# Merging the transfers of a transfer-bound LoRA projection, and sending three small stores from GpSimd earlier

## Chip, cores, metric

One core of a Trainium2 chip. The metric is the device time of one execution in microseconds, of the slowest core (here the only one). Lower is better. The profile's span, from the first to the last instruction, is about 1.3 us shorter than this time.

## The reference

```python
# x: 16 x 2048 x 256, W: 256 x 256, lora_A: 256 x 16, lora_B: 16 x 256, lora_E: 16, scale = 1
x_flat = x.reshape(-1, in_dim)              # 32768 rows of 256 floats
y = x_flat @ W
lora_out = ((x_flat @ lora_A) * lora_E) @ lora_B
return (y + scale * lora_out).reshape(batch, seq_len, out_dim)
```

The kernel folds the low-rank part into one matrix, W + A diag(E) B, and then does one multiplication per row. It must read 33.55 MB of x and write 33.55 MB of y.

## The kernel before

The rows are cut into four chunks of 64 rows on each of 128 partitions, and each chunk into 16 groups of 4 rows. There are three homes in SBUF (chunk 3 goes into the home of chunk 0). For each group GpSimd casts four rows to bf16 (`stage`), TensorE transposes them, VectorE copies the transposed words out, TensorE multiplies, and ScalarE writes the result over the input in the home. The sync engine sends loads and large stores in the order of one list:

```python
ORDER = [
    ("A",),
    ("L", 0, 0, 8), ("L", 0, 8, 24), ("L", 0, 24, 40), ("L", 0, 40, 64),
    ("L", 1, 0, 32), ("L", 1, 32, 64),
    ("L", 2, 0, 16), ("L", 2, 16, 64),
    ("S", 0, 0, 40), ("S", 0, 40, 64),
    ("L", 3, 0, 32), ("L", 3, 32, 64),
    ("S", 1, 0, 64), ("S", 2, 2, 62), ("S", 3, 0, 64),
]
SHARED = 2                       # of chunk 2, the first and last 2 rows ...
SHARES = (slice(108, 113), slice(0, 108), slice(113, P))   # ... go out from GpSimd's queue
HELD = (2, 16)                   # GpSimd holds this group until ...
HOLDERS = (("S", 0, 0, 40),)     # ... this store has landed
```

A store's semaphore makes the load that overwrites its home wait. The end of GpSimd's program and TensorE's loop:

```python
def gpsimd_program():
    # ... identity, then for g in range(N_GROUPS): waits, the hold, and
        gpsimd.tensor_copy(out=stage[g % NS][:], in_=home(c)[:, b:b + CG, :]).then_inc(s_stage[g % UNROLL], 1)

    gpsimd.wait_ge(s_turned, N_GROUPS - NS + 1)
    gpsimd.drain().then_inc(s_stage[N_GROUPS % UNROLL], 1)   # the last release
    gpsimd.wait_ge(s_shared, 1)
    for p in SHARES:
        share(gpsimd, p, shared_stored)                      # a DMA start each

def tensor_program():
    # ...
    with tensor.Fori(0, N_GROUPS // UNROLL):
        for i in range(UNROLL):
            turn(i + 1, i)      # waits for s_stage of group i + 1
            multiply(i)
```

In the loop TensorE transposes group i + 1 before it multiplies group i. After group 63 there is no group 64, yet the loop still does `turn(64)` on old data and throws the result away. The drain, an instruction without data that serves here only to raise a semaphore, is the last release. So **group 63 is multiplied only after the drain has ended**.

Of the kernel before, what the change touches and what calls it, by code (L numbers as in the profile page):

```python
# [16 lines left out]

ORDER = [
    ("A",),
    ("L", 0, 0, 8),  # L20
    ("L", 0, 8, 24),
    ("L", 0, 24, 40),
    ("L", 0, 40, 64),
    ("L", 1, 0, 32),
    ("L", 1, 32, 64),
    ("L", 2, 0, 16),
    ("L", 2, 16, 64),
    ("S", 0, 0, 40),
    ("S", 0, 40, 64),
    ("L", 3, 0, 32),  # L30
    ("L", 3, 32, 64),
    ("S", 1, 0, 64),
    ("S", 2, 2, 62),
    ("S", 3, 0, 64),
]

SHARED = 2
END_ROWS = 2
SHARES = (slice(108, 113), slice(0, 108), slice(113, P))

HELD = (2, 16)
HOLDERS = (("S", 0, 0, 40),)

WARM_UP = 2

EARLIER = 5

CG = 4
GPC = ROWS // CG
# [8 lines left out]
def kernel(  # L58
# [41 lines left out]
        for op in ORDER  # L100
        if op[0] == "S" and (op in HOLDERS or op[1] < N_CHUNKS - N_HOMES)
    }
    stored = {op: sem(f"stored_{op[1]}_{op[2]}") for op in ORDER if op in waited}
    s_shared = sem("shared_done")
    shared_stored = sem("shared_stored")
# [13 lines left out]
    def home(c):  # L119
        return homes[c % N_HOMES]  # L120

    sync, gpsimd, scalar, vector, tensor = nc.sync, nc.gpsimd, nc.scalar, nc.vector, nc.tensor
# [41 lines left out]
    def share(engine, p, landed):  # L164
        def ends_of(rows):
            return rows[p].rearrange("p (q b) k -> p q b k", b=END_ROWS)[:, :: ROWS // END_ROWS - 1, :, :]

        engine.dma_start(out=ends_of(y_chunks[SHARED]), in_=ends_of(home(SHARED))).then_inc(landed, 16)  # L168

    def gpsimd_program():  # L170
        gpsimd.memset(ident[:], 0.0).then_inc(s_ident, 1)  # L171
        gpsimd.wait_ge(s_ident, 1)
        gpsimd.affine_select(  # L173
            out=ident[:],
            in_=ident[:],
            compare_op=ALU.not_equal,
            fill=1.0,
            base=0,
            pattern=[[-1, P]],
            channel_multiplier=1,  # L180
        ).then_inc(s_ident, 1)
        for g in range(N_GROUPS):
            c, b = g // GPC, g % GPC * CG
            for op, landed in loaded.items():
                if op[1:3] == (c, b):
                    gpsimd.wait_ge(landed, 16)
            if (c, b) == HELD:
                for op in HOLDERS:
                    gpsimd.wait_ge(stored[op], 16)
            if g >= NS:  # L190
                gpsimd.wait_ge(s_turned, g - NS + 1)  # L191
            gpsimd.tensor_copy(out=stage[g % NS][:], in_=home(c)[:, b:b + CG, :]).then_inc(s_stage[g % UNROLL], 1)  # L192

        gpsimd.wait_ge(s_turned, N_GROUPS - NS + 1)
        gpsimd.drain().then_inc(s_stage[N_GROUPS % UNROLL], 1)
        gpsimd.wait_ge(s_shared, 1)
        for p in SHARES:
            share(gpsimd, p, shared_stored)

    def scalar_program():  # L200
        for name, to, of in (
            ("w", w_sb, W.rearrange("(q t) m -> q t m", t=KT)),
            ("b", b_sb, lora_B),
            ("e", e_sb, lora_E[:, None]),
        ):
            ins = scalar.dma_start(out=to[:], in_=of).then_inc(set_up_loaded[name], 16)
            opening.append(ins.ins.name)
        for g in range(N_GROUPS):
            c, b = g // GPC, g % GPC * CG
            scalar.wait_ge(s_y, g + 1)  # L210
            scalar.copy(out=home(c)[:, b:b + CG, :], in_=psum_y[g % NY][:]).then_inc(s_free[(g + NY) % UNROLL], 1)  # L211
            if (c, b + CG) == (SHARED, ROWS):
                scalar.drain().then_inc(s_shared, 1)
            if g in ends:
                scalar.drain().then_inc(s_done, 1)  # L215

    def vector_program():
        vector.wait_ge(set_up_loaded["e"], 16)
        vector.wait_ge(s_pe_set_up, 1)
        vector.tensor_scalar(  # L220
            out=ate[:],
            in0=psum_y[0][:R, :KT, :P],
            scalar1=e_sb[:],
            scalar2=float(scale),
            op0=ALU.mult,
            op1=ALU.mult,
        ).then_inc(s_ate, 1)
        for g in range(N_GROUPS):
            vector.wait_ge(s_turned, g + 1)
            vector.tensor_copy(out=xt[g % NX][:], in_=psum_xt[g % NT][:].bitcast(BF16)).then_inc(s_xt[g % UNROLL], 1)  # L230
            if g == 0:
                vector.wait_ge(set_up_loaded["w"], 16)
                vector.wait_ge(s_pe_set_up, 2)
                vector.tensor_add(out=weff[:], in0=w_sb[:], in1=psum_y[1][:, :KT, :]).then_inc(s_free[0], 1)  # L234
                vector.drain().then_inc(s_free[1], 1)
                for _ in range(EARLIER):
                    vector.drain()

    def tensor_program():
# [54 lines left out]
    with tc.tile_critical(no_gpsimd_drain=True):  # L294
        sync_program()
        gpsimd_program()
        scalar_program()
        vector_program()
        tensor_program()
# [35 lines left out]
```

## Time and profile before

| | before |
|---|---|
| time, median of 6 runs | 161.64 us (161.13 to 163.21) |
| profiled execution | 160.84 us, span 159.5 us |
| bytes over HBM | 67.4 MB, mean 423 GB/s |
| last cast on GpSimd, last copy on ScalarE | 112.6 us, done at 118.4 us |
| drain on GpSimd | at 113.9 us, 46 ns |
| the three shares: first issue, landing of the last | 114.7 us, 147.4 us |
| first packet of store 3 | 138.5 us |

The page's line for the main queue (q1) and the strip of 40 slices are read in the prediction. The point to keep in mind is that the first packet of store 3 (138.5 us) comes 20 us after the last copy (118.4 us): that is slack in which something may grow unseen.

### The profile page before, as it was taken

Reading aid. Unit: us, or ns where it says so; the run is one execution under the profiler, and the core shown is the slowest. Engines: PE = TensorE matmul, PEld = TensorE weight load, DVE = VectorE, ACT = ScalarE, POOL = GpSimd, SP = SyncE. Lnnn points to the kernel's source line nnn. Section 1 sums busy time; section 2 is a strip of 40 time slices with the busy share of each in tenths; the row PEclk is TensorE's granted clock in tenths of the full one; section 3 lists DMA queues with packets and bytes.
Section 4 is the critical chain, followed back from the end, with each engine's and each line's share of the span. In section 5 each row is a group of like instructions: output and inputs, shape, how many; then the busy total and the mean of one; then the engine's idle time right before and its main releaser. Section 6 shows DMA issues by size and latency. Waiting matters only on the chain.

```text
span 159.5 us, 2034 instructions
## 1 busy us (share of the span) xinstructions
PE 93.8 (59%) x782; PEld 82.4 (52%) x782; DVE 45.4 (28%) x66; ACT 66.1 (41%) x65; POOL 68.8 (43%) x73
## 2 busy tenths in 40 slices
PE   2969969959999990000899999999940000000000
PEld 1349959959999990000789999999930000000000
DVE  0145534525555550000135555555500000000000
ACT  3025775747777772000147777777750000000000
POOL 1537838377777740001557777787620000000000
PEclk9999999999999999655569999999995555555555
DMA  7999999999999997999999999989979979969896
GB/s 257 417 440 466 401 460 394 501 419 394 431 423 542 444 394 320 431 401 436 413 477 411 411 468 435 536 362 427 493 327 480 502 308 484 514 297 540 378 411 263
DMA packets 2739, 67.43 MB, mean 423 GB/s; under 512 B 544, under 2 KB 560, under 8 KB 816
## 3 DMA queue, kind: packets, MB, share of 16 engines
q1 hardware_dynamic: 2304, 66.60, 97.5%
q0 software_dynamic: 224, 0.52, 0.9%
q10 hardware_dynamic: 208, 0.28, 0.5%
q14 instruction: 3, 0.02, 0.0%
HBM read 33.85 MB, written 33.55 MB: 423 GB/s over the span
## 4 chain that ended last, share of the span: by engine, by line
DMA 43%; PE 27%; POOL 1%; ACT 1%; SPq 1%; issue 0%; ACTq 0%; POOLq 0%
DMA out_dram<-home 30%; PE psum_y L259 17%; DMA home<-in_x_dram 12%; PE psum_xt L248 9%; POOL stage L192 1%; ACT home L211 1%; SPq L156 0%; ACTq L215 0%; SPq L330 0%; POOLq L191 0%; SPq L294 0%
## 5 line engine op out<-in xcount | busy, mean ns | idle before, releaser
L211 ACT COPY home<-psum_y 128x1024 f32<-128x1024 f32 x64 | 64.8, 1012 | 50.3 <-PE psum_y L259 50.3
L192 POOL CAST stage<-home 128x1024 bf16<-128x1024 f32 x64 | 66.1, 1040 | 44.8 <-DMA out_dram<-home 17.3
L259 PE MATMUL psum_y<-weff,xt 128*128 128x256 bf16 x512 | 68.1, 277 | 0.0
L230 DVE COPY xt<-psum_xt 128x1024 bf16<-128x1024 bf16 x64 | 44.3, 692 | 62.7 <-PE psum_xt L248 62.6
L259 PEld LDWEIGHTS psum_y<-weff,xt 128*128 128x128 bf16 x512 | 51.0, 100 | 5.8
L248 PE MATMUL psum_xt<-ident,stage 128*128 128x128 f32 x260 | 40.7, 280 | 20.6 <-POOL stage L192 20.2
L248 PEld LDWEIGHTS psum_xt<-ident,stage 128*128 128x128 f32 x260 | 31.3, 145 | 23.4 <-issue 22.0
L272 PE MATMUL psum_y<-ident 128*128 128x512 f32 x4 | 3.8, 1101 | 2.9 <-POOL ident L173 2.9
L272 PEld LDWEIGHTS psum_y<-ident 128*128 128x128 f32 x4 | 1.2, 325 | 3.9 <-POOL ident L173 2.9
L220 DVE TENSOR_SCALAR ate<-psum_y,e_sb 16x256 f32<-16x256 f32 x1 | 0.5, 472 | 7.2 <-PE psum_y L275 7.2
L168 POOL DMA_DIRECT2D out_dram<-home x3 | 2.0, 675 | 1.0 <-PE psum_xt L248 1.0
L211 ACT ACT_TABLE_LOAD x1 | 1.3, 1283 | 2.0 <-SPq L294 2.0
L281 PE MATMUL psum_y<-b_sb,ate 16*128 16x256 f32 x4 | 1.1, 393 | 0.1
L171 POOL MEMSET ident<- 128x128 f32 x1 | 0.2, 204 | 1.7 <-SPq L294 1.7
L275 PEld LDWEIGHTS psum_y<-ident,a_sb 128*16 128x16 f32 x2 | 0.3, 138 | 1.2 <-issue 1.2
L281 PEld LDWEIGHTS psum_y<-b_sb,ate 16*128 16x128 f32 x4 | 0.7, 184 | 0.4 <-issue 0.3
L234 DVE TENSOR_TENSOR weff<-w_sb,psum_y 128x512 bf16<-128x512 f32 x1 | 0.7, 686 | 0.6 <-PE psum_y L281 0.6
L275 PE MATMUL psum_y<-ident,a_sb 128*16 128x128 f32 x2 | 0.6, 421 | 0.0
L173 POOL TENSOR_SCALAR_AFFINE_SELECT ident<-ident 128x128 f32<-128x128 f32 x1 | 0.3, 283 | 0.2 <-POOL ident L171 0.2
L316 POOL MEMSET const-float32-0.0<- 128x1 f32 x1 | 0.1, 93 | 0.2 <-issue 0.2
L316 POOL MEMSET const-bfloat16-1.0<- 128x1 bf16 x1 | 0.1, 95 | 0.0
L316 POOL MEMSET const-uint8-127<- 128x1 uint8 x1 | 0.1, 95 | 0.0
(1 smaller groups left out, 0.1 us busy)
## 6 DMA issues: line engine op xcount, KB each, us to landing
home<-in_x_dram SPq DMA_DIRECT2D x4, 4096.0 KB, 24.2
out_dram<-home SPq DMA_DIRECT2D x1, 7680.0 KB, 42.3
home<-in_x_dram SPq DMA_DIRECT2D x3, 2048.0 KB, 13.0
home<-in_x_dram SPq DMA_DIRECT2D x1, 6144.0 KB, 58.2
out_dram<-home SPq DMA_DIRECT2D x1, 5120.0 KB, 48.3
home<-in_x_dram SPq DMA_DIRECT2D x1, 3072.0 KB, 19.9
out_dram<-home SPq DMA_DIRECT2D x1, 3072.0 KB, 45.9
home<-in_x_dram SPq DMA_DIRECT2D x1, 1024.0 KB, 5.4
```

The source lines that it names most:

```text
L168: engine.dma_start(out=ends_of(y_chunks[SHARED]), in_=ends_of(home(SHARED))).then_inc(landed, 16)
L192: gpsimd.tensor_copy(out=stage[g % NS][:], in_=home(c)[:, b:b + CG, :]).then_inc(s_stage[g % UNROLL], 1)
L211: scalar.copy(out=home(c)[:, b:b + CG, :], in_=psum_y[g % NY][:]).then_inc(s_free[(g + NY) % UNROLL], 1)
L220: vector.tensor_scalar(out=ate[:], in0=psum_y[0][:R, :KT, :P], scalar1=e_sb[:], scalar2=float(scale), op0=ALU.mult, op1=ALU.mult,).then_in ...
L230: vector.tensor_copy(out=xt[g % NX][:], in_=psum_xt[g % NT][:].bitcast(BF16)).then_inc(s_xt[g % UNROLL], 1)
L234: vector.tensor_add(out=weff[:], in0=w_sb[:], in1=psum_y[1][:, :KT, :]).then_inc(s_free[0], 1)
L248: ins = tensor.transpose(psum_xt[i % NT][:, b, :], words[:, b, :], ident[:])
L259: ins = tensor.matmul(psum_y[i % NY][:, b, :], xt[i % NX][:, b, t::KT], weff[:, t, :], start=(t == 0), stop=(t == KT - 1),)
L272: tensor.matmul(psum_y[1][:, :2, :], ident[:], ident[:, None, :].to_broadcast([P, 4, P]), start=True, stop=True)
L275: ins = tensor.transpose(psum_y[0][:R, t, :P], a_sb[:, t, :], ident[:])
L281: ins = tensor.matmul(psum_y[1][:, t, :], ate[:, t, :], b_sb[:], start=True, stop=True)
L316: nc = _bacc.Bacc("TRN2", target_bir_lowering=False, num_devices=1)
```

## The change

The intent, as far as the change shows it, is to send as few transfers as fit: fewer and larger loads, store 0 whole, 24 rows of store 1 ahead of load 3 to keep the queue fed while load 3 waits for store 0. The three shares go out in the middle of chunk 3, not at the end. Some drains shift the places of the instruction fetches.

```diff
 ORDER = [
     ("A",),
-    ("L", 0, 0, 8),
-    ("L", 0, 8, 24),
-    ("L", 0, 24, 40),
+    ("L", 0, 0, 16),
+    ("L", 0, 16, 40),
     ("L", 0, 40, 64),
     ("L", 1, 0, 32),
     ("L", 1, 32, 64),
-    ("L", 2, 0, 16),
-    ("L", 2, 16, 64),
-    ("S", 0, 0, 40),
-    ("S", 0, 40, 64),
-    ("L", 3, 0, 32),
-    ("L", 3, 32, 64),
-    ("S", 1, 0, 64),
+    ("L", 2, 0, 64),
+    ("S", 0, 0, 64),
+    ("S", 1, 0, 24),
+    ("L", 3, 0, 64),
+    ("S", 1, 24, 64),
     ("S", 2, 2, 62),
     ("S", 3, 0, 64),
 ]
+SHARED_AT = (3, 16)
-HELD = (2, 16)
-HOLDERS = (("S", 0, 0, 40),)
+HELD = (2, 0)
+HOLDERS = (("S", 0, 0, 64),)
-EARLIER = 5
+VECTOR_DRAINS = 9
+GPSIMD_DRAINS = 7
+SCALAR_DRAINS = 15
# (cut: one loop of drains each at the start of GpSimd and ScalarE; VectorE's loop had 5)
@@ gpsimd_program
+            if (c, b) == SHARED_AT:
+                gpsimd.wait_ge(s_shared, 1)
+                for p in SHARES:
+                    share(gpsimd, p, shared_stored)
             if g >= NS:
                 gpsimd.wait_ge(s_turned, g - NS + 1)
             gpsimd.tensor_copy(...)

         gpsimd.wait_ge(s_turned, N_GROUPS - NS + 1)
         gpsimd.drain().then_inc(s_stage[N_GROUPS % UNROLL], 1)
-        gpsimd.wait_ge(s_shared, 1)
-        for p in SHARES:
-            share(gpsimd, p, shared_stored)
```

The order on GpSimd: before, drain and then shares; after, shares and then drain.

More of the change, by code (lines that the diff above doesn't have):

```diff
@@ L181, in gpsimd_program @@
         ).then_inc(s_ident, 1)
+        for _ in range(GPSIMD_DRAINS):
+            gpsimd.drain()
         for g in range(N_GROUPS):
@@ L207, in scalar_program @@
             opening.append(ins.ins.name)
+        for _ in range(SCALAR_DRAINS):
+            scalar.drain()
         for g in range(N_GROUPS):
@@ L235, in vector_program @@
                 vector.drain().then_inc(s_free[1], 1)
-                for _ in range(EARLIER):
+                for _ in range(VECTOR_DRAINS):
                     vector.drain()
```

## The prediction

> **What bounds the kernel now.** I read the page's queue table first, then the strip of 40 slices, then the chain of waits, then the table by stage, then the sync engine's own waits and GpSimd's timeline.
>
> ```profile
> DMA packets 2739, 67.43 MB, mean 423 GB/s; under 512 B 544, under 2 KB 560, under 8 KB 816
> q1 hardware_dynamic: 2304, 66.60, 97.5%
> HBM read 33.85 MB, written 33.55 MB: 423 GB/s over the span
> ...
> DMA  7999999999999997999999999989979979969896
> ```
>
> 33.55 MB of x must come in and 33.55 MB of y go out. The main queue alone fills 97.5% of the time of 16 DMA engines. The digits below 9 in the strip are mostly an artefact, since a long packet is counted in the slice where it starts. Laying the packet records of the trace on one clock, I find 15 to 16 or more packets in flight at every instant from 2.0 us to 158.4 us of a 159.5 us span. No engine of DMA is idle between those two times. So the kernel is bound by transfer time and nothing else; compute matters only if it makes a transfer start late.
>
> ```profile
> core 0: us, PE busy (x) PEld busy (x) DVE busy (x) ACT busy (x) POOL busy (x), PEclk, DMA share, GB/s
> ...
> 2.00:20.00 18.00, 15.78 (x101) 11.34 (x102) 6.69 (x10) 7.43 (x8) 10.53 (x12) 1.00 1.02 428
> 20.00:58.00 38.00, 34.82 (x318) 31.96 (x316) 17.99 (x27) 26.69 (x27) 26.95 (x27) 1.00 1.02 442
> 58.00:62.00 4.00, 2.14 (x20) 1.71 (x18) 1.38 (x2) 2.59 (x3) 0.00 (x0) 1.00 1.00 342
> 62.00:80.00 18.00, 3.74 (x18) 3.15 (x19) 0.74 (x2) 0.91 (x1) 3.09 (x4) 0.59 0.97 417
> 80.00:99.00 19.00, 19.00 (x166) 17.42 (x165) 9.63 (x14) 13.26 (x14) 14.30 (x14) 0.94 1.00 432
> ```
>
> The DMA share (last but one column) stays near 1 in every stage, whether TensorE is busy or idle. One stage is poor in bytes: 342 GB/s at 58 to 62 us, where the first store follows the last load of chunk 2. There the trace shows some 17 packets of 49152 B taking 2.4 to 2.9 us instead of 1.82; the excess of that size group, divided by 16, is 0.86 us. The later changes between loads and stores (at 81 and 100 us) show next to none.
>
> ```profile
> SPq L156 <- DMA out_dram<-home: 38.3, 1, 38.3
> POOL stage L192 <- DMA out_dram<-home: 17.3, 1, 17.3
> ...
> 75.08 2.02 POOL L192 CAST stage<-home 128x1024 bf16<-128x1024 f32 x2 [17.32 <-DMA out_dram<-home]
> 112.61 1.04 POOL L192 CAST stage<-home 128x1024 bf16<-128x1024 f32 x1 [0.27 <-PE psum_xt L248]
> 114.69 2.02 POOL L168 DMA_DIRECT2D out_dram<-home  x3 [1.04 <-PE psum_xt L248]
> ```
>
> The long waits are deliberate or harmless. GpSimd holds chunk 2 for 17.3 us until the first store has landed (74.97 us), and the sync engine waits for the same store before it sends the first load of chunk 3 into that home. Meanwhile the second store of chunk 0 (24 rows) keeps the queue fed. The chain of waits runs through these holds and through TensorE (27%), but TensorE finishes at 117.4 us, and the last store's first packets start at 138.5 us: some 20 us of slack that the share in the chain hides.
>
> **What the Trainium skill says.** "DMA: Bandwidth & Descriptors", section "Where 436 GB/s comes from", puts the ceiling of the SBUF ports at 435 GB/s. The trace agrees: a 65536 B packet takes 2418 ns, 27.1 B/ns, or 434 GB/s for 16 engines; the 358 GB/s that the page gives as the HBM limit does not bind here (mean 423). The same page, section "Anatomy of one DMA", gives a fixed cost of about 2 us per DMA, mostly the wait for the completion receipt. That is no queue time here: packets of consecutive transfers follow each other without a hole, so merging transfers saves descriptor overhead, not 2 us each. Section "Queues, rings and completion order" says each engine takes its queues in turn, packet by packet; the trace agrees, the GpSimd queue's 4096 B packets start 2.42 us apart on each engine, one after each 61440 B packet (2267 + 159 ns). "TensorE: Matmul & The Clock Gate", section "What's actually happening", has the clock halve after an idle window and recover after some 3.4 us of work; the trace shows half clock from 65.2 to 82.2 us, with work resumed at 76.3, so about 6 us to recover here.
>
> **The change, part by part.**
>
> Removed: three transfers of the main queue. Before has four loads of chunk 0, two each of chunks 1, 2 and 3, and five stores, 15; after has 3 + 2 + 1 + 1 loads and 5 stores, 12. Each transfer gives every engine 8 packets, one per partition, and one semaphore write. Durations in the trace: 309 ns for 8192 B, 611 for 16384, 1213 for 32768, 2418 for 65536. The slope is (2418 - 309) / 57344 = 0.0368 ns per byte, so 8192 B are 301 ns and the fixed part of a packet is 8 ns. Per transfer and engine: 8 x 8 ns + 9 ns (the 4 B write) = 0.07 us. Three fewer: 0.21 us, all of it on the bound.
>
> Start: the first load doubles from 8 to 16 rows. Its first packet still starts at about 2.0 us. The first 8-row load loses 0.22 us per engine to company (packets of up to 662 ns instead of 309), mostly the weights' packets; some of that company's cost may go, I take 0.05 us. Compute begins later by 8 rows x 0.30 us = 2.4 us; nothing waits for it, since the first store is due only when the loads end at about 61 us.
>
> Moved: store 0 whole, then 24 rows of store 1 ahead of load 3. I lay the queue out with 0.3015 us a row (64 rows: 8 x 2.418 = 19.3 us). Loads 0 to 2 end at about 61.1 us (if the 0.86 us stays). Store 0 ends at 80.5 and lands at about 80.9. The 24 rows last 24 x 0.3015 = 7.2 us, to 87.8. Load 3 waits for store 0's landing, so it is sent at about 81 with nearly 7 us to spare, the same margin as now. Its end is 107.1; the 40 rows of store 1 end at 119.2, store 2's 60 rows at about 137.5, and store 3 follows.
>
> Compute has to fit into this. Chunk 2 is released at 80.9 instead of having four groups done early. The four first casts at half clock cost 82.48 - 75.08 = 7.4 us, the rest 1.31 us each: the 16th cast starts at 80.9 + 7.4 + 11 x 1.31 = 102.7, and its result is in SBUF 5.8 us later (as 112.61 to 118.4 now), at 108.5. Store 2 is due at 119.2: 10 us to spare. Chunk 3 lands at about 107.5. Sixteen groups: three casts in 3.1, twelve steps of 1.31 (15.7), plus the three shares now sent by GpSimd in the middle (2.0 us, and 0.8 before it as now between the drain at 113.9 and the first at 114.7), plus 5.8: 107.5 + 3.1 + 15.7 + 2.8 + 5.8 = 134.9. Store 3 is due when the first engine gets there, about 137.5 to 138.5. So the slack shrinks from 20 us to about 3, yet stays above zero.
>
> The shares' packets now start at about 114 instead of 119.6; they are the same 128 packets (1.4 us per engine in the mean) and still end well before the end.
>
> Drains: 15 on ScalarE, 7 on GpSimd, 4 more on VectorE (10 ns each there, issued 40 ns apart). All stand in stretches where these engines wait for loads; cost zero. They move the instruction stream, and so the three 8192 B instruction fetches at 61.7, 80.0 and 102.7 us. Each costs one engine 309 ns; at most the engine that ends last gains that.
>
> Sum: -0.21 - 0.05 - about 0.1 for fetches and the end's unevenness (the engines' last packets end between 158.4 and 159.15 us) = about -0.35 us of 159.5. I set it against 161.66, whose three runs lie at 161.13, 161.66 and 163.21, so its middle may be high by 0.1: 161.2 us.
>
> **The rivals.** First, a hole before store 3, because slack falls to 3 us: if the clock stays halved through chunk 3 (2.5 us a group instead of 1.31), its results come about 19 us late and the time grows by some 15 us, to 177. Against it: TensorE pauses only about 1 to 3 us between chunks 2 and 3, and the trace keeps full clock through a 2.9 us wait for a load at 32.6 us. A milder form, 1 to 2 us late, makes 162 to 163. Second, the slow changeover at 58 to 62 us vanishes or grows with 65536 B packets and a whole store: without it, the time is 160.3. For this: the later changeovers cost nothing. Against it: it belongs to the first store, which comes in the same place after the same loads. Third, a different spread over the engines: in before, one engine's eight packets of store 1 take 2564 ns each, 146 more than the rest, 1.2 us in all, which the uneven shares seem to make good. If after has the slowness on another engine, the end moves by up to 1.2 us, to 162.4.
>
> **Range and chances.** The bound is 67.1 MB at 434 GB/s, 154.6 us, and the fixed start (2.0), end and launch (1.3 us between time and span) leave no road to 158.4, which 2% faster would need: 0.01. Slower by over 2% needs a hole of 3.2 us: 0.03. The range is the run-to-run spread plus rivals two and three: 160.1 to 162.5.
>
> **What would show it.** The main queue should have 2304 - 3 x 144 = 1872 packets (128 data and 16 semaphore writes each). DMA packets should stay in flight without a hole from 2 to 158 us; TensorE's last matmul should fall at about 134 and the last store's issue before 137; the hold on GpSimd should run to about 81 us. A pause of the queue around 87 us (load 3 late) or 138 us (store 3 late) would prove me wrong on the slack; a DMA rate near 430 GB/s around 60 us would show that the changeover went.

## The result, and the profile after

The changed kernel takes 167.47 us (median of 6, 167.21 to 168.01) against 161.64 us: **ratio 1.0354**, 95% interval 1.0309 to 1.0399, slower. A ratio here is the mean time of one kernel's fast runs over that of the other's fast runs of the same rounds, so it is not quite the ratio of the medians quoted. The prediction was 161.2 us with a range to 162.5.

First the page's queue lines and the strip, after:

```profile
DMA packets 2307, 67.43 MB, mean 406 GB/s; under 512 B 496, under 2 KB 512, under 8 KB 768
q1 hardware_dynamic: 1872, 66.60, 93.8%
...
DMA  7999998989799796999799799889998992099595
GB/s 276 436 432 432 420 474 387 489 387 568 316 505 505 286 458 300 474 489 442 322 414 592 302 474 489 367 385 454 508 414 352 497 483 92 0 505 505 253 505 253
```

The packets are exactly the 1872 predicted, and the bytes are the same. But the main queue's share falls from 97.5% to 93.8%, and slices 34 and 35 of the strip (a slice is 4.15 us) show 92 and 0 GB/s. The transfers stop when store 2 has ended. The table by stage gives the place; first before, then after (the last two columns are the DMA share and GB/s):

```profile
138.00:140.00 2.00, 0.00 (x0) 0.00 (x0) 0.00 (x0) 0.00 (x0) 0.00 (x0) 0.50 1.35 574
140.00:146.00 6.00, 0.00 (x0) 0.00 (x0) 0.00 (x0) 0.00 (x0) 0.00 (x0) 0.50 0.85 360
```

```profile
138.00:140.00 2.00, 0.00 (x0) 0.00 (x0) 0.00 (x0) 0.00 (x0) 0.00 (x0) 0.75 0.40 158
140.00:146.00 6.00, 2.79 (x12) 1.92 (x12) 0.00 (x0) 1.01 (x1) 0.00 (x0) 0.50 0.00 1
146.00:164.00 18.00, 0.00 (x0) 0.00 (x0) 0.00 (x0) 0.00 (x0) 0.00 (x0) 0.50 1.08 466
```

From 140 to 146 us next to nothing is moved (1 GB/s), and TensorE does 12 matmuls: the 4 transposes of the pass that is thrown away and the 8 products of group 63. Nearly everywhere else the packet records again show 16 or more in flight. Summed over the time from 138 to 148 us, the 16 DMA engines stand idle 6.5 us each in the mean, which is the whole difference of the spans (166.0 - 159.5). So the question is what holds the last group back. The chain of waits of the changed kernel, in that window (start, duration, what):

```profile
132.87 0.87 PE psum_y L264 x8
133.74 0.45 PE psum_xt L253 x4
134.19 7.03 POOLq L201
141.22 0.14 issue
141.36 1.09 PE psum_xt L253 x4
142.45 1.72 PE psum_y L264 x8
144.17 0.02 issue
144.19 1.01 ACT home L216
```

L201 is the drain on GpSimd. The chain puts 7.03 us on it. By the timeline TensorE's last other product, of group 62, ended at 135.06 us, and TensorE then sat idle for 6.31 us. Then come the pass that is thrown away, the product of group 63 (both at half clock by now: 1.72 us against 0.87 for the product), ScalarE's copy, and store 3, sent at 145.26 us into an empty queue. The same line looked at by itself, after and then before:

```profile
L201 POOLq DRAIN  x1: 8308/8308/8308, 132.9 to 132.9; - x1
...
  PE psum_xt L253: 6.3, 1
```

```profile
L195 POOLq DRAIN  x1: 46/46/46, 113.9 to 113.9; - x1
```

The drain grew from 46 ns to 8308 ns. By the Trainium skill, "Perfetto Trace Analysis", section "Per-engine timelines", the profiled time of a drain starts only when its semaphores are satisfied. The trace agrees: it starts at 132.91 us, when TensorE has done the transposes that it was told to wait for. So the 8.3 us are not the wait written in the program. What ends them is next to them in the trace: the last of the 48 increments of the shares' semaphore comes at 141.04 us, and the drain ends at 141.22.

### The profile page after: what moved, and what is told of

Its sections match the earlier page's. It is cut to its first block, busy times and chain, and to the rows that moved or that the text cites. A ratio compares the mean times of both kernels' runs of the same rounds, so it can differ in the third digit from the quotient of the medians.

```text
span 166.0 us, 2053 instructions
## 1 busy us (share of the span) xinstructions
PE 98.2 (59%) x782; PEld 85.2 (51%) x782; DVE 45.4 (27%) x66; ACT 66.1 (40%) x65; POOL 69.0 (42%) x73
## 3 DMA queue, kind: packets, MB, share of 16 engines
q1 hardware_dynamic: 1872, 66.60, 93.8%
## 4 chain that ended last, share of the span: by engine, by line
DMA 49%; PE 29%; POOLq 4%; POOL 4%; ACT 1%; issue 1%; SPq 0%; ACTq 0%
DMA out_dram<-home 28%; DMA home<-in_x_dram 21%; PE psum_y L264 17%; PE psum_xt L253 11%; POOLq L201 4%; POOL stage L198 3%; ACT home L216 1%; PE psum_y L286 1%; POOL out_dram L168 1%; SPq L147 0%; ACTq L220 0%
## 5 line engine op out<-in xcount | busy, mean ns | idle before, releaser
L264 PE MATMUL psum_y<-weff,xt 128*128 128x256 bf16 x512 | 70.2, 283 | 0.0
L253 PE MATMUL psum_xt<-ident,stage 128*128 128x128 f32 x260 | 42.9, 291 | 43.1 <-POOL stage L198 36.8
L253 PEld LDWEIGHTS psum_xt<-ident,stage 128*128 128x128 f32 x260 | 32.6, 150 | 46.3 <-issue 45.0
L264 PEld LDWEIGHTS psum_y<-weff,xt 128*128 128x128 bf16 x512 | 52.1, 102 | 6.8
L286 PE MATMUL psum_y<-b_sb,ate 16*128 16x256 f32 x4 | 2.1, 670 | 0.0
L286 PEld LDWEIGHTS psum_y<-b_sb,ate 16*128 16x128 f32 x4 | 1.2, 320 | 0.5 <-issue 0.3
```

The lines of the kernel that those rows point to most:

```text
L253: ins = tensor.transpose(psum_xt[i % NT][:, b, :], words[:, b, :], ident[:])
L264: ins = tensor.matmul(psum_y[i % NY][:, b, :], xt[i % NX][:, b, t::KT], weff[:, t, :], start=(t == 0), stop=(t == KT - 1),)
L286: ins = tensor.matmul(psum_y[1][:, t, :], ate[:, t, :], b_sb[:], start=True, stop=True)
```

## The experiments

Theory A: GpSimd's drain waits until the transfers that GpSimd itself has started have landed. Theory B: whatever GpSimd runs after starting transfers is held. Theory C: the drain is a symptom, and holding chunk 2 until the whole of store 0 has landed leaves too little slack. All kernels gave correct results. "Before" had medians of 161.46 us (e1 to e4) and 161.48 (e5 to e8).

**e1: the release by a memset.**

```diff
# changed kernel
+    scratch = sbuf("scratch", [P, 1], FP32)
-        gpsimd.drain().then_inc(s_stage[N_GROUPS % UNROLL], 1)
+        gpsimd.memset(scratch[:], 0.0).then_inc(s_stage[N_GROUPS % UNROLL], 1)
```

> The changed kernel with one instruction replaced: GpSimd's last release (the one that lets TensorE run its last pass) is a memset of 128x1 in place of the drain. Theory A, the drain waits until GpSimd's own share transfers have landed (141.04 us in the trace, the drain ends at 141.22): the release falls at about 133 us, the last copy ends at about 136.6, store 3 is in the queue before store 2 ends (about 139), the hole is gone, time 160.8 to 161.4. Theory B, anything that GpSimd runs after its transfers is held by them: memset held too, 167.4. Theory C, the slack was simply too small because chunk 2 is held longer: a hole stays, 163 or more.

162.12 us (161.20 to 162.37), ratio to before 1.0024 (0.9987 to 1.0061): the loss is gone. The memset's line, then the stages at the place of the hole:

```profile
L202 POOL MEMSET scratch<- x1: 98/98/98, 132.8 to 132.8; 128x1 f32 x1
```

```profile
138.00:140.00 2.00, 0.00 (x0) 0.00 (x0) 0.00 (x0) 0.00 (x0) 0.00 (x0) 1.00 0.97 408
140.00:146.00 6.00, 0.00 (x0) 0.00 (x0) 0.00 (x0) 0.00 (x0) 0.00 (x0) 0.55 0.98 420
```

The memset runs at 132.84 us, while the shares land at 141.81. B falls, and C falls as an explanation of this loss: with all of the new order kept, the queue has no hole (15 or more packets in flight from 2 to 157 us). The time is 0.7 us above the expected upper bound; see the last part of this section.

**e2: the shares after the drain again.** All else as changed.

```diff
# changed kernel
-            if (c, b) == SHARED_AT:
-                gpsimd.wait_ge(s_shared, 1)
-                for p in SHARES:
-                    share(gpsimd, p, shared_stored)
 ...
         gpsimd.drain().then_inc(s_stage[N_GROUPS % UNROLL], 1)
+        gpsimd.wait_ge(s_shared, 1)
+        for p in SHARES:
+            share(gpsimd, p, shared_stored)
```

> The changed kernel with the three share transfers sent after the drain again, as before the change; all else (order of transfers, drain counts, hold) as changed. Theory A: drain of 0.05 us, hole gone, about 161.0; the shares land near 150 to 155 us, ahead of the end. Theory C: GpSimd saves only the 2 to 3 us that the shares took in the middle, so time stays above 164.

162.04 us, ratio 1.0026 (0.9992 to 1.0061). The drain takes 39 ns at 131.2 us; the last share lands at 159.45, close to the end of store 3 and not at 150 to 155 us as I had expected, and the time is 1.0 us above the expected one. The new order of loads and stores, the longer hold and the added drains together are thus within noise of before.

**e3: the kernel before, with the shares early and nothing else.**

```diff
# kernel before
+SHARED_AT = (3, 16)
+            if (c, b) == SHARED_AT:            # in the loop over groups, as in the change
+                gpsimd.wait_ge(s_shared, 1)
+                for p in SHARES:
+                    share(gpsimd, p, shared_stored)
 ...
         gpsimd.drain().then_inc(s_stage[N_GROUPS % UNROLL], 1)
-        gpsimd.wait_ge(s_shared, 1)
-        for p in SHARES:
-            share(gpsimd, p, shared_stored)
```

> The kernel before with the shares sent after four groups of chunk 3 and the drain after them, nothing else. Theory A: the drain, now at about 116 us, is as long as the shares are still under way (until about 122 to 128 us), yet store 3 is due only at 138.5, so the time stays within 0.5 of 161.6. Theory B or C: drain of 0.05 us, or no drain effect; same time. The length of the drain, not the time, tells them apart.

161.91 us, ratio 1.0012 (0.9961 to 1.0063). Its drain:

```profile
L200 POOLq DRAIN  x1: 20593/20593/20593, 115.2 to 115.2; - x1
...
  PE psum_xt L250: 18.6, 1
```

The drain takes **20.6 us**, more than twice that of the changed kernel, and the time does not move clear of noise: the last copy ends at 139.80 us, just about when store 3 falls due. The 20 us of slack are used up and a little more: by the packet records of this trace the first packet of store 3 starts at 140.69 us, and the 16 DMA engines stand idle for 1.0 us each in the mean before it. The shares were under way until 135.64, longer than the 122 to 128 us that I had expected, and the drain ended at 135.81, again 0.18 us after. So the moved shares cost at most about 1 us here, which four runs don't tell from nothing, and 5 us in the changed kernel, because the kernel before has 20 us of slack before store 3.

**e4: the shares three groups sooner.** `SHARED_AT = (3, 4)` in the changed kernel.

> The changed kernel with the shares sent after one group of chunk 3 instead of four, so about 4 us sooner. Theory A: they find shorter packets (40960 B) to alternate with and land at about 132 to 136 us, so the drain is 0 to 3 us and the time 161 to 163. Theory C: nothing gained, 167 or more.

166.67 us, ratio 1.0313: a miss. The drain is shorter, as A says, but the end hardly moves:

```profile
L201 POOLq DRAIN  x1: 4462/4462/4462, 136.4 to 136.4; - x1
```

Two things went against the estimate. The shares' first packets started 5 us after their first issue (113.7 and 118.7 us), too late for the short packets of store 1; they alternated with store 2's 61440 B packets, 2.43 us a turn, and landed at 140.66, only 0.4 us sooner than in the changed kernel. And GpSimd waited 4.0 us for the end of chunk 2 before it could send them, which delayed chunk 3. The drain ended at 140.83, 0.18 us after the landing, as in the changed kernel.

**e5: the shares from another engine's queue.**

```diff
# changed kernel; GpSimd's block of shares removed, its drain kept
 def scalar_program():
         for g in range(N_GROUPS):
             c, b = g // GPC, g % GPC * CG
+            if (c, b) == SHARED_AT:
+                scalar.wait_ge(s_shared, 1)
+                for p in SHARES:
+                    share(scalar, p, shared_stored)
             scalar.wait_ge(s_y, g + 1)
```

> The changed kernel, its drain kept, but the three shares sent from ScalarE's queue (just before its copy of the fifth group of chunk 3, about 117 us) and not from GpSimd's. Theory A in its narrow form, GpSimd's drain waits for the transfers that GpSimd itself sent: drain of about 0.05 us at 130 to 131 us though the shares are still under way until about 139, hole gone, 161 to 163. Theory A in a wide form, the drain waits for any transfer in flight that is not the sync engine's: drain of 8 us or more and about 167.

GpSimd's drain, and the issue of the shares on ScalarE's queue:

```profile
L197 POOLq DRAIN  x1: 34/34/34, 133.9 to 133.9; - x1
```

```profile
L168 ACTq DMA_DIRECT2D out_dram<-home x3: 537/592/936, 121.1 to 122.3; - x3
```

The shares are under way from 121.1 to 142.9 us, and GpSimd's drain at 133.9 takes 34 ns. So the drain waits for transfers that GpSimd started, not for any transfer in flight. ScalarE's own drain at 137.4 us took 1.04 us, no longer than behind its other copies, with its three transfers still under way. The time was 163.41 us, ratio 1.0106 (1.0058 to 1.0153), above my 161 to 163. There is hardly a hole (12 or more packets in flight, 0.12 us of idle in the mean), but one DMA engine ends its part of store 3 at 161.84 us while the middle one ends at 159.47. Why that one is late stays open.

**e6: e1, and chunk 2 loaded in 48 and 16 rows.** `("L", 2, 0, 48), ("L", 2, 48, 64)` in place of `("L", 2, 0, 64)`.

> The changed kernel with the memset release, and chunk 2 loaded as 48 and 16 rows, so that the last packets before the first store are of 16384 B and not 65536 B. In the traces so far the packets that lie over this change from loads to stores are late by 0.85 us in the mean of 16 queues with 49152 B packets and by 0.94 to 1.23 with 65536 B. If the excess grows with the size of the packet, it falls below 0.5 and the time to about 161.2; if it is a fixed cost of the first store, it stays near 0.9 and the time at 161.9.

161.86 us, ratio 1.0014 (0.9975 to 1.0052). The packets at the first change from loads to stores are late by 0.79 us per DMA engine in the mean. Over all runs it is 0.79 with 16384 B packets, 0.85 to 0.87 with 49152 B, and 0.91 to 1.32 with 65536 B. That is nearer to a fixed cost than to one in proportion to the packet, and the time is the one expected for a fixed cost (161.9); the times do not tell e6 from e1.

**e7: the drain counts alone**, in the kernel before (9 on VectorE, 7 on GpSimd, 15 on ScalarE).

> The kernel before with the drain counts of the change alone (9 on VectorE, 7 on GpSimd, 15 on ScalarE). By my prediction they stand where the engines wait for loads and cost nothing: 161.5, within 0.5% of before. If they hold the start, 0.5 us more or longer.

161.82 us, ratio 1.0022 (0.9978 to 1.0066): no effect that can be seen.

**e8: e1 with the wait put back in the open.**

```diff
# kernel e1
+        gpsimd.wait_ge(shared_stored, 16 * len(SHARES))
         gpsimd.memset(scratch[:], 0.0).then_inc(s_stage[N_GROUPS % UNROLL], 1)
```

> The changed kernel with the memset release, but GpSimd first waits on the semaphore of the three shares, so the wait that theory A sees inside the drain is put back openly. Theory A: the release comes at the shares' landing (about 141 us), the hole is back, 167.0 to 167.6, as in the changed kernel. If the drain held for another reason: the shares would be seen to land well before 141 and the time would fall short of 166.

167.86 us, ratio 1.0379 (1.0330 to 1.0428), 0.3 us above the range that I had expected: the loss is back in full, without any drain at that place. The chain:

```profile
116.26 25.16 DMA out_dram<-home
141.42 0.02 issue
141.44 0.02 POOLq L202
141.46 0.07 issue
141.53 0.11 POOL scratch L203
```

**What the repaired kernels leave open.** e1, e2 and e6 lie 0.14 to 0.26% above before, with intervals that include 1, where I had expected e1 and e2 0.2 to 0.3% below. In the single traces of e1 and e2 the 16 DMA engines end their last packets over 2.0 and 1.3 us, against 0.7 us in the trace of before, and one late engine sets the end. But e7, which moves no transfer, shows a spread of 1.6 us too, so the spread may belong to the run and not to the kernel. What inside GpSimd keeps its drain until the landing, no run shows. No version here beats the kernel before.

## Why the prediction was wrong

- **The bound: right.** Transfer time bounds both kernels; without the hole the packet records show the queue full from 2 to 158 us (e1).
- **The removed transfers: right in number, not seen in time.** The queue has 1872 packets as computed. The 0.21 us they should save is below what the runs tell apart, and the changeover and the end took at least as much in the traces. (The 2 us per DMA that the prediction quotes from "Anatomy of one DMA" stand there under the path from GpSimd; the prediction counted none of it, so nothing in the sum rests on it.)
- **The moved shares: here the prediction failed.** It counted them as the "same 128 packets" that "still end well before the end", and charged GpSimd 2.8 us for sending them. It took no account of the drain that now stands behind them in GpSimd's program, nor of `turn(64)`, which ties the last product to that drain. It used the drain at 113.9 us only as a mark in time; the 46 ns that the drain took there were measured with nothing under way from GpSimd. Nor did the shares get out earlier: the prediction had their packets start at about 114 us, but chunk 3 came later than it thought and the first packet starts only 4.55 us after the first issue, so they started at 120.47, where before had 119.64. The move changed only their place ahead of the drain. The missing term is a wait until the shares' landing: 8.3 us of drain, 6.5 us of hole.
- **The last result: put 2.4 us too early.** I put it at 134.9 us; without the drain's wait (e1) the last copy ends at 137.3. The error lies in the landing of chunk 3, not in the compute after it. In e1 it landed at 110.90 us and not at 107.5, and from there to the last copy took 26.4 us where I had 27.4. Part of the lateness is that a landing waits for the slowest of 16 engines, while I had reckoned with the mean: in the changed kernel store 0's 16 increments came from 81.23 to 82.87 us (I had 80.9), and load 3's from 107.84 to 110.20. The slack that I gave as about 3 us was about 1: e1 sends store 3 at 137.38 and its first packet starts when the queue comes to it, at 139.38; the way from issue to packet takes 0.84 us (145.26 to 146.10 in the changed kernel), which leaves 1.2. Rival one (a hole before store 3) named the right place, but for a clock that stays at half, and I set it aside by asking about TensorE alone. That answer was itself misread: the 2.9 us at 32.6 us was GpSimd's wait, while TensorE paused 1.66 us there; between chunks 2 and 3 it paused 4.1 us in e1, not 1 to 3, and its clock did fall to half, for 3.4 us. In the real case the late instruction was on GpSimd.
- **Rival two (the slow changeover): it stayed**, as I chose; 1.17 us in the trace after, 0.85 before.
- **Why 5.3 us and not 6.5.** Removing the wait (e1) brings 167.47 to 162.12, and the spans 166.0 to 161.0, not to 159.5. In the trace after, the hole also evens out the engines: they all start store 3 together at 146.1 and end within 0.16 us, while in e1 one engine ends 1.35 us after the middle one.

The size of the loss fits: against e1 the release comes 8.4 us later (141.22 against 132.84), the last copy ends 7.9 us later (145.20 against 137.32), and the first packet of store 3 starts 6.7 us later (146.10 against 139.38), since the slack of 1.2 us is used up first.

## What to carry to other kernels

When a transfer is moved ahead of other work on the engine that starts it, look at every drain that now follows it and at who waits for that drain: the drain's 46 ns in the profile of before was not a fixed price; it grew to 8.3 us once GpSimd's own transfers were under way ahead of it. If a release carries no data, give it to an instruction that did not wait for transfers here, such as the memset of e1 (98 ns). And a wait of 20 us in a place with 20 us of slack (e3) hardly shows in the time until another part of the same change has used the slack up; so test the parts in the kernel in which they will stand.

## What the Trainium skill lacked or had wrong

- No page says that a drain on GpSimd waits for transfers. "GPSIMD Engine Reference" says nothing of what a drain waits for; of drains in general, "PSUM — Partial Sum Buffer" says only that one waits for the engine to go fully idle. Here a drain on GpSimd lasted until 0.18 us after the landing of the transfers that GpSimd had started: 8308, 4462 and 20593 ns in three kernels, against 34 to 46 ns with none of its own under way (in e5 with the same transfers under way from ScalarE's queue, in before with the sync engine's queue full).
- "Perfetto Trace Analysis", section "Per-engine timelines", treats a drain as a sequencer's instruction that executes once its semaphores are satisfied. The start agrees; the execution here was up to 20.6 us, and the page names nothing that it could wait for.
- "DMA: Bandwidth & Descriptors", section "Latency and other measured facts", gives about 1 us to the first byte for transfers from GpSimd. Here, beside a full main queue, the first 4096 B packet started 4.5 to 5.1 us after the first of three issues (114.69 to 119.64 in before, 115.92 to 120.47 in the changed kernel). How long it takes into an empty queue, no run here shows.
- No page has the cost of the first change from loads to stores: 0.8 to 1.3 us per DMA engine in every trace here, 0.5 us or less at the later changes.
